# One loop body with staggered semaphore resets in place of 16 unrolled repeats, in a DMA-bound log-softmax gradient

One NeuronCore of a Trainium2 chip. The metric is the device time of one execution in microseconds, the median of several; times are compared within one chip.

## What is computed

```python
# y, dy: (8, 1024, 8192) float32
softmax_x = np.exp(y)
sum_dy = np.sum(dy, axis=-1, keepdims=True)
return dy - softmax_x * sum_dy
```

The 8192 rows are taken as 32 groups. In a group each of 128 partitions holds 2 neighbouring rows of 8192 elements, 64 KB, so one group of one tensor is a transfer of 8.39 MB. The kernel reads 537 MB and writes 268 MB.

## The kernel before

Two groups make a repeat, and there are 16 repeats, written out by a Python loop. Group g works in buffer x0, group g + 1 in x1. The y of the first lies in the upper part of one buffer y_t, the y of the second in its lower part, which overlaps the first. All transfers are issued by SyncE, in this order.

```python
def load_dy(g, x):
    nc.sync.dma_start(out=x[:], in_=dy_v[g])

def load_y(g, at, lo, hi):
    nc.sync.dma_start(out=y_t[:, at + lo : at + hi], in_=y_v[g][:, lo:hi])

# sums(x): VectorE sums row 0 of each partition, ScalarE row 1
# compute(...): in three pieces a row, ScalarE exp in y_t, VectorE x = y_t * s + x

for g in range(0, G, 2):
    load_dy(g, x_ts[0])                       # x0      64 KB a partition
    load_y(g, SHIFT, 0, W)                    # y       64 KB
    s_t = sums(x_ts[0])
    for r in range(R):
        compute(x_ts[0], s_t, SHIFT, r, PIECES_A)
    load_dy(g + 1, x_ts[1])                   # x1      64 KB
    s_t = sums(x_ts[1])
    for r in range(R):
        load_y(g + 1, 0, r * D, (r + 1) * D)  # first, second half of y, 32 KB each
        compute(x_ts[1], s_t, 0, r, PIECES_B)
    for j in range(2):
        nc.sync.dma_start(out=out_v[g + j], in_=x_ts[j][:])   # store of x0, store of x1
# ... cut: shapes, pools, launch
```

## Time and profile before

| | before |
|---|---|
| time | 1867.33 us (1866.91 to 1867.59, 4 runs) |
| bytes through the data queue | 805.31 MB, 432 GB/s over the span |
| busy share of VectorE, ScalarE | 46%, 37% |
| share of the 16 DMA engines' span that packets took | 99.8% |

Read it from the bottom row up: where the DMA engines have no idle time, the busy shares of the compute engines say nothing about the time, and the question for any change is whether it lets the DMA queue run dry. The lines are in the prediction.

Beside the views, the trace holds every DMA packet (start, duration, size). A row of 64 KB is one packet, and each of the 16 DMA engines carries 8 rows of a transfer. A packet does not name its engine: I follow an engine from the end of one packet to the start of the next, and a transfer's end on each engine is marked by a packet of 4 bytes. From these I work out, for each transfer, what the engines lost in it: the time from the end of the transfer before to its own end, mean over the engines, less what an undisturbed transfer takes (19.32 us with rows of 64 KB, 9.68 us with rows of 32 KB). This number, "lost in a transfer", is used throughout. In the kernel before it is 0.18 us for a whole repeat (repeats 1 to 14).

### The profile page before, as it was taken

The page shows a single profiled execution, that of the slowest core. Times are in us where ns is not written, and L with a number is a line of the kernel's source. Part 1 is how long each engine was busy: PE and PEld are TensorE (multiplying, and loading weights), DVE is VectorE, ACT ScalarE, POOL GpSimd, SP SyncE. Part 2 cuts the span into 40 slices and gives each one's busy share as a digit, 9 for nine tenths or more (in the row PEclk, how much of TensorE's full clock was granted, in tenths as well). Part 3 has the DMA queues.
Part 4 walks back from the last instruction along what each step waited for, and adds up shares of the span by engine and source line. Part 5 has one row for each costly group of instructions (what it writes and reads, how often), then busy time and mean ns, then how long its engine had stood idle before and what let it go on. Part 6 is the DMA issues. An engine that isn't in the chain of part 4 may idle for free.

```text
span 1866.1 us, 843 instructions
## 1 busy us (share of the span) xinstructions
DVE 857.9 (46%) x256; ACT 689.3 (37%) x257; POOL 0.2 (0%) x4
## 2 busy tenths in 40 slices
DVE  2907429074290742807328073280732806338163
ACT  2606326063260532605326053260523605235152
POOL 0000000000000000000000000000000000000000
DMA  9999999999999999999999999999999999999998
GB/s 427 427 427 427 431 444 429 427 434 443 427 434 438 425 435 442 428 429 431 440 431 430 438 427 436 437 440 427 430 438 435 428 437 428 438 435 434 434 428 386
DMA packets 16134, 805.36 MB, mean 432 GB/s; under 512 B 1792, under 2 KB 1792, under 8 KB 1792
## 3 DMA queue, kind: packets, MB, share of 16 engines
q1 hardware_dynamic: 16128, 805.31, 99.8%
q14 instruction: 6, 0.05, 0.0%
HBM read 536.87 MB, written 268.44 MB: 432 GB/s over the span
## 4 chain that ended last, share of the span: by engine, by line
DMA 65%; DVE 14%; another core or an unknown queue 10%; ACT 9%; issue 0%; DVEq 0%; ACTq 0%; SPq 0%
DMA x<-in_dy_dram 31%; DMA out_dram<-x 30%; DVE x L74 14%; ACT x L60 6%; ACT y_t L73 3%; DMA y_t<-in_y_dram 3%; DVEq L121 0%; ACTq L121 0%; SPq L52 0%; ACTq L73 0%; ACTq L60 0%
## 5 line engine op out<-in xcount | busy, mean ns | idle before, releaser
L74 DVE SCALAR_TENSOR_TENSOR x<-y_t,s_t,x 128x1024 f32<-128x1024 f32 (+2 forms) x192 | 579.4, 3059 | 257.5 <-ACT y_t L73 257.5
L57 DVE TENSOR_REDUCE s_t<-x 128x1 f32<-128x8192 f32 x32 | 277.8, 8682 | 721.9 <-DMA x<-in_dy_dram 721.9
L73 ACT ACTIVATE y_t<-y_t 128x1024 f32<-128x1024 f32 (+2 forms) x192 | 460.1, 2466 | 280.0 <-DMA y_t<-in_y_dram 280.0
L60 ACT ACTIVATE x<-x 128x8192 f32<-128x8192 f32 x32 | 225.0, 7030 | 863.2 <-DMA x<-in_dy_dram 863.2
L60 ACT ACTIVATION_READ_ACCUMULATOR x<-x 128x1 f32 x32 | 6.0, 187 | 0.0
L61 DVE TENSOR_SCALAR s_t<-second_t 128x1 f32<-128x1 f32 x32 | 4.6, 143 | 0.0
L60 ACT ACT_TABLE_LOAD x1 | 1.3, 1283 | 0.7 <-PEq L110 0.7
L110 POOL MEMSET const-uint8-127<- 128x1 uint8 x1 | 0.1, 102 | 0.0
L110 POOL MEMSET const-bfloat16-1.0<- 128x1 bf16 x1 | 0.1, 101 | 0.0
L110 POOL MEMSET const-float32-0.0<- 128x1 f32 x1 | 0.1, 98 | 0.2 <-issue 0.2
L110 POOL MEMSET const-float32-1.0<- 128x1 f32 x1 | 0.1, 98 | 0.0
## 6 DMA issues: line engine op xcount, KB each, us to landing
y_t<-in_y_dram SPq DMA_DIRECT2D x32, 4096.0 KB, 22.1
x<-in_dy_dram SPq DMA_DIRECT2D x32, 48.4
out_dram<-x SPq DMA_DIRECT2D x32, 32.6
y_t<-in_y_dram SPq DMA_DIRECT2D x16, 57.5
```

The lines of the kernel that those rows point to most:

```text
L57: nc.vector.tensor_reduce(out=s_t[:, 0:1], in_=x[:, :D], axis=mybir.AxisListType.X, op=ALU.add, negate=True)
L60: nc.scalar.activation(x[:, D:], x[:, D:], COPY, accum_out=second_t[:])
L61: nc.vector.tensor_scalar(out=s_t[:, 1:2], in0=second_t[:], scalar1=-1.0, scalar2=None, op0=ALU.mult)
L73: nc.scalar.activation(y_t[:, ys], y_t[:, ys], EXP)
L74: nc.vector.scalar_tensor_tensor(out=x[:, xs], in0=y_t[:, ys], scalar=s_t[:, r : r + 1], in1=x[:, xs], op0=ALU.mult, op1=ALU.add,)
L110: nc = _bacc.Bacc("TRN2", target_bir_lowering=False, num_devices=1)
```

## The change

The 16 repeats become one body, repeated by a branch on a register. Semaphores are reset stage by stage while the engines run: the body has four stages, and no engine enters a stage before all have reported the stage two back as done. The two `previous_stage_wait` lines make ScalarE and VectorE report one stage earlier than they otherwise would. The intent is a program of about a sixteenth of the length that runs as fast.

```diff
-    for g in range(0, G, 2):
+    with tc.For_i(0, G, 2, iteration_sync="staggered") as g:
         load_dy(g, x_ts[0])
         load_y(g, SHIFT, 0, W)
+        tc.stage_boundary()
+
+        for engine in (mybir.EngineType.Activation, mybir.EngineType.DVE):
+            tc.previous_stage_wait(engine)
         s_t = sums(x_ts[0])
         for r in range(R):
             compute(x_ts[0], s_t, SHIFT, r, PIECES_A)
         load_dy(g + 1, x_ts[1])
+        tc.stage_boundary()
+        for engine in (mybir.EngineType.Activation, mybir.EngineType.DVE):
+            tc.previous_stage_wait(engine)
         s_t = sums(x_ts[1])
         for r in range(R):
             load_y(g + 1, 0, r * D, (r + 1) * D)
             compute(x_ts[1], s_t, 0, r, PIECES_B)
+        tc.stage_boundary()
         for j in range(2):
             nc.sync.dma_start(out=out_v[g + j], in_=x_ts[j][:])
```

What the diff does not show, and the built program does: the store of x1 now waits for the semaphore that the store of x0 raises when it has landed.

## The prediction

> **What bounds the kernel now.** I read the page first (spans, slices, queues), then the DMA queue's own waits, then the timeline of one repeat, then the chain.
>
> ```profile
> span 1866.1 us, 843 instructions
> DVE 857.9 (46%) x256; ACT 689.3 (37%) x257; POOL 0.2 (0%) x4
> DMA  9999999999999999999999999999999999999998
> ...
> q1 hardware_dynamic: 16128, 805.31, 99.8%
> ```
>
> No engine is half busy, and the DMA row is 9 in all slices but the last; the one data queue's packets fill 99.8% of the 16 DMA engines' span. 805.31 MB in 1866 us is 432 GB/s. So the kernel is bound by the DMA engines, and only something that lets them go idle, or changes the bytes, can move the time. The bytes stay.
>
> One repeat (two groups) moves 6 x 8.39 MB: dy into x0, y, dy into x1, two half loads of y, store of x0, store of x1. All go through one queue, in the order of issue. In the trace's DMA packets a 64 KB row takes 2.418 us on its engine and the next starts at once (2.414 us from start to start), so an 8.39 MB transfer (8 rows per engine) takes 8 x 2.414 = 19.3 us. Six are 115.9 us; consecutive repeats in the trace end 116.06 to 116.9 us apart (the first later). The rest are small stalls that hit all engines at once.
>
> What matters is how early each transfer is queued before the one ahead of it runs out:
>
> ```profile
> 166.63 9.25 SPq L67 DMA_DIRECT2D y_t<-in_y_dram  x2
> ...
> 179.69 30.23 SPq L95 DMA_DIRECT2D out_dram<-x  x2
> ...
> 217.48 0.34 SPq L52 DMA_DIRECT2D x<-in_dy_dram  x1
> ...
> 236.90 0.33 SPq L52 DMA_DIRECT2D x<-in_dy_dram  x1
> ```
>
> This is the timeline of the second repeat, SyncE alone (start, duration, and two issues merged in a row). The store of x0 is issued at 179.69, the store of x1 ends its issue at 179.69 + 30.23 = 209.92. The next load of x0 starts at 217.48, released by the landing of the store of x0. So the store of x1 stood in the queue 7.6 us before its predecessor landed. It is the smallest reserve of the repeat. For the others: the first half of y is queued at 166.63 and the load ahead of it lands about 178.2 (11.6 us); the load of x0 is queued at 217.48 and the store ahead lands at 236.90 (19.4 us).
>
> ```profile
> SPq L67 <- DMA y_t<-in_y_dram: 615.0, 16, 39.7
> SPq L95 <- DVE x L74: 526.6, 32, 30.0
> SPq L52 <- DMA out_dram<-x: 386.4, 30, 18.5
> SPq L67 <- DVE x L74: 260.4, 32, 8.6
> ```
>
> These are the queue's own waits. **All 32 stores wait for VectorE**, none for a DMA: no store waits for another. The 30 waits on a store are loads into a buffer that is still being written out.
>
> The chain shows that these waits follow one another with no hole that the DMA engines feel:
>
> ```profile
> 62.52 38.28 DMA out_dram<-x
> 100.81 0.02 issue
> 100.82 38.71 DMA x<-in_dy_dram
> ```
>
> **What the Trainium skill says.**
> - "DMA: Bandwidth & Descriptors", Anatomy of one DMA: a DMA costs about 2.0 us fixed beside its bytes (fitted on GpSimd's path), mostly because the semaphore moves only when the last byte is confirmed; DMA engines don't wait on semaphores, the issuing sequencer does. The trace agrees in size: the first load is issued at 0.73 us and its last engine lands at 22.45, 21.72 us for 19.31 us of rows: 2.41 us fixed.
> - Same page, Latency and other measured facts: about 600 ns to the first byte from SyncE. The trace: the issue ends at 0.73 + 0.38 = 1.11, the first packets start at 1.74, 0.63 us later; the last of the 16 engines starts at 2.39.
> - "Advanced Engine Details and Errata", Control Flow Timing: a branch about 51 ns, compare-and-branch about 108 ns. The kernel before has no loop, so its trace can't show it.
> - "Runtime: NRT & Kernel Launch", Instruction fetch mechanics: a taken branch whose target isn't among the two resident blocks of 256 instructions stalls for a fetch. The loop body is some 20 to 40 instructions per engine, so I expect none after the first pass.
>
> **The change part by part.** The built program of the changed kernel holds the body once, with the same operations and shapes in the same order per engine and per queue. It adds:
>
> (a) *Loop control.* Per repeat and engine one add, one compare-and-branch, about ten semaphore instructions, an address instruction ahead of each of SyncE's DMAs. On SyncE the branch lies right after the store of x1 is issued, with a whole 19.3 us transfer running: free. On ScalarE and VectorE it lies between the end of one repeat's work (about 209 us in the timeline above) and 256 us, when x0 has landed: free. ScalarE's table load moves into the loop, 16 x 1.28 us (one in the page now, 1283 ns), in the same idle stretch: free. Before the first DMA there is one more barrier and a few semaphore sets: I put 1 us for it, once, a guess.
>
> (b) *Stage waits.* SyncE may not enter a stage until all engines have reported two stages back. Load of x1 after both stores have landed: the store of x1 it waited for anyway. Half loads of y after x0 and y have landed and after ScalarE and VectorE have reported stage 0, which the change makes them do at the head of stage 1; so the half loads still wait for VectorE's second piece. (If they reported only at the head of stage 2, the load would slip by some 13 us and eat its 11.6 us reserve. That is what this placement is for.) Stores after x1 has landed and both engines have finished x0: both were so before (178.2, and 179.7 for VectorE). So nothing here is on the path: 0 us.
>
> (c) *One new wait.* In the built program the store of x1 waits for the full count (16) of the semaphore that the store of x0, just ahead, raises. It didn't before. I read it as caution: with a register as group number the two destinations can't be told apart. So the store of x1 is issued only when the store of x0 has landed. At that moment nothing else is queued: the reserve goes from 7.6 us to below zero, and all 16 DMA engines run dry once per repeat.
>
> Cost of one dry spell, on the engine that ends last: last packet's end to its landing, 0.36 us (store of x0 in the first two repeats: 0.367 and 0.361); waking SyncE 0.02 us (an "issue" row above) and one more instruction between wait and issue, about 0.1; issue to the last engine's first packet, 2.39 - 0.73 = 1.66 us; filling the pipeline, 0.39 us (that engine's first row took 2.81 instead of 2.42). Sum 2.5 us if a store starts as the first load did. A store reads from SBUF and may fill faster, by up to the 0.39 us, and the first DMA of a program may be colder: 2.1 to 2.5. Against it, engines that drift apart (0.4 us apart in the first repeat, 1.1 us by the fourth) now wait for the slowest every repeat: 0.1 more. I take **2.4 us x 16 repeats = 38 us**. It is not hidden: VectorE is done 7.6 us earlier.
>
> Sum: 1867.5 + 38 + 1 = **1906 us**, 2.1% more.
>
> **The rivals.**
> - *Everything hidden.* If the new wait costs no more than a fraction of a microsecond (engines refilled quickly, say 0.6 us), 16 x 0.6 + 1 gives 1878 us. For it: 99.8% busy, and all stage waits have reserves. Against it: the queue can't be refilled before the landing, and the trace's only start from idle cost 2.4 us.
> - *A stage wait becomes the path.* If reports come later than I read them, the half loads of y slip to VectorE's end of x0: 1 to 2 us more per repeat, together 1920 to 1940 us. Against it: the order of decrement and wait in the built program.
> - *Branch fetches or slower address set-up* on SyncE, some us per repeat: they lie behind a 19.3 us transfer, so no change (1906), except set-up between landing and issue; 0.5 us there would give 1914.
> - *A gain:* a shorter program fetches fewer instructions, but the page's instruction queue has 0.05 MB in all, 0.0% of the time. Nothing to win.
>
> **Range and chances.** The sum hangs on one figure, 16 times the dry spell. 1.9 us gives 1899, 2.9 us gives 1915; with a little for the rest the range is 1896 to 1917. The 2% line is at 1867.5 x 1.02 = 1904.8, a dry spell of 2.27 us, just below my 2.4. So slower by over 2% has 0.58, within 2% 0.41, faster 0.01.
>
> **What would show it right or wrong.** Right: the queue's own waits show half of the stores' waits on a store rather than on VectorE, about 6 to 8 us each (from VectorE's end of x1 to the landing); the data queue's share falls from 99.8% to about 97.9%; in the packets all engines are idle together about 2 us between the two stores and nowhere else; repeats are about 118.5 us apart; busy times of VectorE and ScalarE unchanged but for 16 table loads. Wrong: a second idle stretch elsewhere in the repeat, above all ahead of the half loads of y (a stage wait); or no idle stretch between the stores (the wait isn't the bound); or the idle stretch is there but well under 2 us, and the kernel stays within 2%.

## The result

1919.18 us (1918.63 to 1919.38, 4 runs) against 1867.33: 2.8% slower. The ratio is 1.0277, 95% interval 1.026 to 1.0295. The predicted range ended at 1917.

The page of the changed kernel:

```profile
span 1917.4 us, 2048 instructions
DVE 859.4 (45%) x256; ACT 708.6 (37%) x272; POOL 0.2 (0%) x4
DMA  9999999999999999999999999999999999999999
...
q1 hardware_dynamic: 16128, 805.31, 98.5%
```

Same bytes, same work on VectorE; ScalarE has 16 table loads now (15 x 1.28 = 19.2 us more). The DMA row still shows 9 everywhere: a slice is 48 us wide, and a hole of 1.3 us in it can't be seen. The queue's share is the line that tells, and it fell only from 99.8% to 98.5%, while the time rose by 2.8%. So idle time is about half of the loss, and the other half hides in packets that took longer.

The queue's own waits (line of the waiting instruction, what ended the wait, us in total, times, longest):

```profile
SPq L83 <- DMA y_t<-in_y_dram: 608.3, 16, 39.3
SPq L103 <- DMA out_dram<-x: 598.0, 16, 37.7
SPq L83 <- DMA out_dram<-x: 284.9, 15, 19.1
SPq L67 <- DVE x L74: 250.8, 32, 8.4
SPq L83 <- DMA x<-in_dy_dram: 38.5, 16, 2.4
```

L103 is the stores. Before, all 32 of them waited for VectorE; now 16 wait 37 us each for a store. That wait runs from the issue of the store of x0 to its landing, so it swallows the one for VectorE. The L83 waits are the stage entries.

SyncE in the second repeat, and with it VectorE's last two pieces of x1 (timeline):

```profile
184.10 38.28 SPq L103 DMA_DIRECT2D out_dram<-x  x2
...
207.25 6.75 DVE L74 SCALAR_TENSOR_TENSOR x<-y_t,s_t,x 128x3072 f32<-128x3072 f32 x2 [0.30 <-ACT y_t L73]
...
223.14 0.35 SPq L52 DMA_DIRECT2D x<-in_dy_dram  x1
223.68 1.11 SPq L67 DMA_DIRECT2D y_t<-in_y_dram  x1
```

The pair of stores stretches from 184.10 to 222.38; before it ended 7.6 us ahead of the landing. VectorE is done with x1 at 214.0, 8 us before the store is issued. The chain through the same place (start, duration, what):

```profile
184.10 37.79 DMA out_dram<-x
221.89 0.02 issue
...
222.02 0.35 SPq L103
222.38 0.05 issue
...
222.90 0.03 SPq L129
...
223.14 40.02 DMA x<-in_dy_dram
```

It reads as a ledger of the dry spell, that is, the stretch in which the queue holds nothing and the engines idle. The store of x0 lands at 221.89, SyncE issues the store of x1 at 222.02, and between 222.38 and 223.14 lie the stage entry, the reset and the branches back to the head of the loop, 0.76 us in all, behind a transfer that is already queued. In the packets, the last engine ends the store of x0 at 221.54 and the first engine starts the store of x1 at 222.87: 1.33 us in which all 16 are idle. There is one such stretch in each of the 16 repeats (1.31 to 1.34 us), and nowhere else.

What was lost in each transfer, from the packets, ns, mean of repeats 1 to 14:

```
                 x0   y   x1  first half  second half  store x0  store x1   sum
before           12   5   26      23           99          8         2      175
changed         132  -2   -2      -1          885         -2      2579     3590
```

The difference is 3.4 us a repeat in these 14, and 51.9 us in the whole execution. 2.6 us is lost in the store of x1, as the dry spell would have it. But 0.8 us more is lost in the second half load of y, which is queued long before it starts and has no wait near it: the last two of its 8 rows on an engine take 1.50 and 1.80 us on average, where the others take 1.21. The prediction has nothing there.

The store of x1 itself is not made up as I thought either. Of its 2.58 us, 1.75 are the gap from one store's end to the next one's start on an engine (the 1.33 us, and the wait for the slowest engine), 0.1 lies in its first seven rows, and 0.72 in its **last** row. That row stalls where the engines turn from storing to loading, as the second half of y stalls where they turn from loading to storing. In the last repeat, where no load follows, the store of x1 lost 1.78 us instead.

### The profile page after: what moved, and what is told of

The parts are those of the page before. It is cut to its first block, busy times and chain, and to the rows that moved or that the text cites. A ratio compares the mean times of both kernels' runs of the same rounds, so it can differ in the third digit from the quotient of the medians.

```text
span 1917.4 us, 2048 instructions
## 1 busy us (share of the span) xinstructions
DVE 859.4 (45%) x256; ACT 708.6 (37%) x272; POOL 0.2 (0%) x4
## 3 DMA queue, kind: packets, MB, share of 16 engines
q1 hardware_dynamic: 16128, 805.31, 98.5%
## 4 chain that ended last, share of the span: by engine, by line
DMA 64%; another core or an unknown queue 11%; DVE 11%; ACT 8%; issue 3%; SPq 1%; ACTq 0%
DMA x<-in_dy_dram 31%; DMA out_dram<-x 30%; DVE x L74 11%; ACT x L60 6%; DMA y_t<-in_y_dram 3%; ACT y_t L73 3%; SPq L103 0%; SPq L67 0%; SPq L83 0%; SPq L52 0%; SPq L129 0%; ACTq L73 0%
```

## The experiments

Six questions, fifteen runs. All results were correct.

### Is the new wait the whole loss?

The loop without it. The two stores never touch the same rows, so the dependency may be declared away.

```diff
-        for j in range(2):
-            nc.sync.dma_start(out=out_v[g + j], in_=x_ts[j][:])
+        st = [nc.sync.dma_start(out=out_v[g + j], in_=x_ts[j][:]) for j in range(2)]
+        tc.declare_no_dep(st[1].ins, st[0].ins, reason="rows of group g + 1 are not rows of group g")
```

> The loop with one dependency declared away, so the store of x1 no longer waits for the landing of the store of x0; nothing else changes. Theory (the new wait is the whole loss): 1868 to 1870 us, that is the kernel before plus about 1.2 us for the later first issue (1.97 instead of 0.73 us); no stretch with all DMA engines idle; the stall at the end of the second half load of y shrinks over the first three repeats as it does before. Rival (the stage waits, semaphore resets or address instructions cost by themselves, the 0.9 us stall among them): 16 x 0.9 more, about 1883 us or above.

Measured 1867.87 us against 1867.34 for the kernel before on the same chip, ratio 1.0003 (0.9989 to 1.0016). Its page and the queue's waits:

```profile
span 1866.1 us, 2032 instructions
...
SPq L102 <- DVE x L74: 459.5, 16, 29.4
...
SPq L67 <- DVE x L74: 250.8, 32, 8.4
```

The stores wait for VectorE again, and all the rest of the loop (stage waits, resets, address instructions, branches, 16 table loads) costs nothing that these runs can show. The loss in the second half load is 0.54 us in repeat 0, 0.17 to 0.27 in repeats 1 to 7, and 0.03 from repeat 10 on. Its mean over repeats 1 to 14 is 0.13 us, against 0.10 in the kernel before and 0.89 in the changed one: it went with the wait.

The counter-test is the kernel before, unrolled, with that wait added and SyncE's order pinned (shortened; the loads are pinned too).

```diff
+        st = [tc.keep_in_program_order(nc.sync.dma_start(...)) for j in range(2)]
+        tc.add_manual_dep(st[1].ins, st[0].ins.name, <Sync>, reason=...)
```

> The unrolled kernel before, with SyncE's order pinned and one dependency added: the store of x1 waits for the landing of the store of x0. No loop. Theory (the wait is the whole loss, the stalls beside the idle stretch follow from it): 1917 to 1919 us, an idle stretch of 1.3 us per repeat, 2.5 us lost in the store of x1 and 0.9 us in the second half load of y in every repeat. Rival (only the 2.5 us come from the wait, the 0.9 us from the loop): 1905 to 1908 us.

Measured 1918.83 us, ratio 1.0274 (1.026 to 1.0288): the loop's time with no loop. Lost per repeat: 2.66 us in the store of x1, 0.88 us in the second half load. Its waits show the same pattern as the loop's:

```profile
SPq L97 <- DMA out_dram<-x: 607.1, 16, 39.1
SPq L52 <- DMA out_dram<-x: 300.0, 15, 20.2
```

**What follows.** The wait is necessary and enough for the whole loss, the part in the second half load included. The rival, that the loop's own instructions cause the 0.9 us, is out.

### Does the stall in the half load follow from the dry spell before it?

The same, with the wait in repeats 4, 8 and 12 alone (`if g in (8, 16, 24)` around the added dependency).

> As the last, but the wait stands in repeats 4, 8 and 12 alone (counted from 0). Theory (a dry queue puts the 16 DMA engines back in step, and in step they stall where they turn from loads to stores, until they have drifted apart): the second half load of y loses 0.8 to 1.0 us in repeats 5, 9 and 13, then less in the two after each; time 1867.3 + 3 x (2.5 + 1.3) = 1878 to 1880 us. Rival (the stall belongs to a dry spell of the same repeat or to the loop): no stall in repeats 5, 9, 13; 1875 us or less.

Measured 1878.67 us. Lost in the second half load of y and in the store of x1, ns, by repeat:

```
repeat         0   1   2   3     4    5   6   7     8     9  10  11    12   13   14   15
second half  780  56 206  93   208  972 195  24    43  1021  32  97    79  895  404  269
store x1      -2   7  -1  -2  2914   -2  43   4  2788    -2   4   1  4408   -2   -2   -2
```

Each dry spell is followed, a repeat later, by a stall of 0.9 to 1.0 us in the second half load, which is 0.03 to 0.40 us in the next. Repeat 0, which also starts from idle, has it too. So one dry spell costs itself and a stall some 97 us later; (1878.67 - 1867.34) / 3 is 3.8 us each.

### Does the wait cost anything where the queue is not empty?

The unrolled kernel with the wait, SyncE's order left to the scheduler, which puts the next repeat's whole load of y between the two stores.

> Unrolled, with the same wait of the store of x1 in every repeat, but the scheduler is left free and puts the next repeat's whole load of y ahead of that store, so 19.3 us of transfer stand in the queue while the store of x0 lands. Theory (the wait costs only because nothing is queued behind the store of x0): 1867 to 1870 us with one dry spell, at the end of the last repeat. Rival (a wait of a store on a store costs in itself, wherever it stands): 1900 us or more.

Measured 1884.03 us. SyncE in its third repeat (timeline):

```profile
305.74 0.34 SPq L94 DMA_DIRECT2D out_dram<-x  x1
332.32 0.33 SPq L67 DMA_DIRECT2D y_t<-in_y_dram  x1
337.64 0.34 SPq L94 DMA_DIRECT2D out_dram<-x  x1
```

The load of y is queued at 332.32, the store of x0 lands at 337.6 and releases the store of x1, and 19.3 us of y stand before it. The packets show a single all-idle stretch, at the end of the last repeat, so the wait as such is harmless; that half of the expectation held. But 17 us are lost all the same, so the other half, the time, failed. The packets place it: 1.06 us a repeat in the early load of y, at its turn into the store of x1, and 0.35 us more than before in the two half loads. The order now turns between loads and stores four times a repeat instead of twice. To tell order from wait, the same order without the wait (shortened: at the head of a repeat the load of y stays in the first repeat alone, and SyncE's order is pinned):

```diff
         for j in range(2):
+            if j and g + 2 < G:
+                load_y(g + 2, SHIFT, 0, W)
             nc.sync.dma_start(out=out_v[g + j], in_=x_ts[j][:])
```

> The order of flat_wait_y_first (next load of y ahead of the store of x1) without the wait. Theory: the 17 us that flat_wait_y_first lost come from its order, which turns between loads and stores four times a repeat instead of twice, and not from the wait: 1880 to 1886 us here too. Rival (the 17 us are the wait's): 1867 to 1870 us.

Measured 1882.53 us: so some 15 of the 17 us belong to the order. That turn lost 0.91 us on average, between 0.25 and 1.48 by repeat, in a queue that never ran dry. And with the early load in two halves:

> As flat_y_first, the early load of y in two halves of 32 KB rows. It asks whether the length of the rows ahead of the turn sets the stall (1.1 us before the store of x1 with 64 KB rows against 0.1 to 0.4 before the store of x0 with 32 KB rows, in flat_wait_y_first): if so, about 1870 to 1875 us; if not, the same as flat_y_first.

Measured 1871.01 us, and 0.07 us lost at that turn. Short rows ahead of this turn took the stall away, in this queue without dry spells.

### What does a dry spell cost by itself?

The store of x1 in two halves, the second waiting for the first.

> Unrolled, the store of x1 in two halves, the second waiting for the first as the first waits for the store of x0: two dry spells per repeat. The second adds idle time and restart alone, since the turn stalls are there already: 1.7 to 1.9 us each (1.3 all idle plus the engines' spread), so 1918.8 + 16 x 1.8 = 1947 us, 1943 to 1952. If a dry spell of a store after a store cost the whole 3.2 us that the loop lost, it would be 1970.

Measured 1945.69 us: (1945.69 - 1918.83) / 16 = 1.68 us for a second dry spell (another chip, whose kernel before took 1867.64 against 1867.34). That is the price of one wait for a landing with nothing queued behind, without the turns: the 1.3 us all idle and the engines' spread.

### What are the early reports worth?

The loop without the wait, and without the two `previous_stage_wait` pairs.

> The loop without the wait between the stores, and without the two early reports, so that ScalarE and VectorE report a stage done only two stages on. The half loads of y then wait for VectorE's end of x0 (about 179.7 in the timeline of before, 1.5 us after the load ahead has landed) and the store of x0 waits for VectorE's end of x1 (about 11 us after the second half load of y). I expect two dry spells per repeat, about 3 us and about 13 us, so 16 x 16 to 17 us more: 2120 to 2150 us. If the placement of the reports didn't matter it would stay at 1868 us.

Measured 2027.87 us, 8.6% slower. One of my two dry spells is there, and it is 9.1 us instead of 13; the other is not. The timeline of the second repeat:

```profile
169.64 14.32 ACT L73 ACTIVATE y_t<-y_t 128x1024 f32<-128x1024 f32 x6 [12.23 <-DMA y_t<-in_y_dram]
184.40 2.17 SPq L67 DMA_DIRECT2D y_t<-in_y_dram  x2
...
208.47 7.22 ACT L73 ACTIVATE y_t<-y_t 128x2048 f32<-128x2048 f32 x3 [2.55 <-DMA y_t<-in_y_dram]
...
216.12 4.08 SPq L98 DMA_DIRECT2D out_dram<-x  x2
```

The half loads are issued at 184.40, when **ScalarE** has ended x0 (183.96), not VectorE, and x1 lands only at about 189: a reserve of 4.6 us is left. The store of x0 is issued at 216.12, just after ScalarE has ended x1 (215.69). The engines ran out of work at 207.9 and restart at 217.0. So the reports' place matters, for the store more than for the half loads. In this run the second half load, after which the queue runs dry, lost 0.01 us: without a store right behind it there is no stall.

### Why do the engines stall at a turn?

My reading was that a dry queue puts the 16 DMA engines back in step, and that in step they get in one another's way where they all turn at once. In the kernel before they lie 0.4 us apart in repeat 0 and 3.7 us apart at the end, and the loss at the turn falls from 0.94 to 0.03 us meanwhile (not evenly: 0.37 in repeat 6). To set them apart at the start, one small load ahead of all, on 8 partitions and so on 8 engines:

```diff
+    nc.sync.dma_start(out=x_ts[1][0:8, 0:D], in_=dy_v[1][0:8, 0:D])
     for g in range(0, G, 2):
```

> The kernel before with one 8-partition half-row load at the start, so that 8 engines begin 1.2 us behind. Theory in step: the 0.9 us that the second half load of y loses in repeat 0, and the 0.4 us in repeat 1, fall to 0.2 us or less; time 1867 +- 1. Rival restart: they stay, time 1868.5.

Measured 1869.82 us, later by the load itself (x0 lands up to 3.6 us later). The second half load took 9.71 us in repeat 0, against 10.64 in the kernel before and 9.68 undisturbed: the stall is gone in this repeat. It isn't in all others: 0.19 us was lost in repeat 3 and 0.35 in repeat 8. Repeat 0 spoke for the reading. Then four attempts to do this after every dry spell, all on the unrolled kernel with the wait, each storing a few rows of x0 once more (the same bytes) ahead of the store of x1 (shortened):

```diff
         st = [ ...store of x0... ]
+        nc.sync.dma_start(out=out_v[g][0:8, 0:D], in_=x_ts[0][0:8, 0:D])   # or fewer columns, or other rows
         st.append( ...store of x1, with the wait... )
```

> Unrolled with the wait in every repeat, and after each dry spell SyncE stores 8 half rows of x0 once more (the same bytes), ahead of the store of x1: an 8-partition transfer should use 8 of the 16 DMA engines, so those run 1.2 us behind the other 8 through the following repeat. Theory in step (the stall at the turn from loads to stores, 0.9 us, and at the end of the store of x1, 0.7 us, come from all engines turning together): both shrink to 0.3 us or less while the idle stretch stays; the 1.2 us is paid once per repeat, so the time is 1910 to 1920 us. Rival restart (the stalls are what a restart from idle costs later, whatever the engines' distance): both stalls stay and 16 x 1.2 us is added, 1935 to 1940 us.

Measured 2001.66 us, a failed test. The rows took some 5.3 us each, not 1.2, and left two blocks of 8 engines some 4 us apart. The second half load lost 0.59 us, where flat_wait lost 0.88. At the turn to loads the last two rows of the store of x1 lost 0.39 us (0.73 in flat_wait), and the load of x0 behind them another 0.39 (0.12).

> As flat_wait_skew, but the extra stores take every fourth partition, so that the rows lie apart in SBUF, and are three: 8, 4 and 2 rows of 16 KB. The engines should then lie 0, 0.6, 1.2 and 1.8 us apart after each dry spell. In flat_wait_skew the 8 neighbouring rows took 5.3 us each instead of 1.2, so that run paid 16 x 5.2 us and left two blocks of 8 engines, each in step: no clean test. Theory in step: the stall at the turn to stores and the one at the end of the store of x1 both fall to 0.4 us or less; 1.8 us per repeat is paid and about 1.2 saved: 1923 to 1933 us. Rival restart: both stalls stay, 1918.8 + 29 = 1945 to 1950 us.

Measured 1957.24 us, a failed test again. The small stores were done before the store of x1 reached the engines, which therefore began it within 0.35 us of one another. The stalls were 0.7 us each, not far below flat_wait's 0.88 and 0.73. One thing this run shows beside its question: its 8 rows of 16 KB, every fourth partition, took 0.61 us each, while 8 neighbouring rows of 16 KB (flat_wait_lag16, below) took 2.3 to 3.0 us.

> As flat_wait_skew with rows of 8 KB instead of 32 KB. There the 8 neighbouring rows took 5.3 us, so here about 1.3 us, less the 0.5 us by which the store of x1 comes later: 8 engines lag the other 8 by about 0.8 us, as in skew_start. Theory in step: the stall at the turn to stores (0.9 us) and at the end of the store of x1 (0.7 us) fall to 0.4 us or less: 1904 to 1914 us. Rival restart: both stay, 1918.8 + 16 x 0.9 = 1930 to 1936 us.

Measured 1946.15 us. The lag was gone by the end of the store of x1 (all 16 engines within 0.55 us in the second repeat): no test.

> The same with rows of 16 KB: 8 engines lag by about 2.1 us. Theory in step: stalls fall to 0.4 us or less each, 1918.8 + 16 x (2.2 - 1.0) = 1938, 1930 to 1942 us. Rival restart: 1918.8 + 35 = 1951 to 1956 us.

Measured 1963.43 us, and here the engines did end the store of x1 in two blocks, at 244.8 to 245.0 and 246.1 to 246.5 us. The turn to stores lost 0.75 us. At the turn to loads the last two rows of the store of x1 lost 0.45 us and the load of x0 behind them 0.41, together what flat_wait lost there (0.73 and 0.12). So distance between two blocks doesn't remove the stalls; at most it moves a part of one. **The reading falls as I stated it.** The other suspect was the length of the rows ahead of the turn, after the run with half loads. With the dry spell kept, the second half load in two transfers of 16 KB rows, and the store of x1 in four:

> flat_wait with the second half load of y in two transfers of 16 KB rows (32 KB before). If the length of the rows ahead of the turn sets the stall, the 0.9 us falls to 0.45 or less: 1918.8 - 16 x 0.5 or more = 1903 to 1911 us, and the 0.7 us at the other turn stays. If row length doesn't matter: 1918 to 1920 us.

Measured 1919.62 us; the loss at the turn is 0.90 us, as with 32 KB.

> flat_wait with the store of x1 in four transfers of 16 KB rows (64 KB before), only the first of them with the wait. If row length sets the stall at the turn from stores to loads, the 0.7 us falls to 0.35 or less: 1907 to 1913 us, and the 0.9 us stays. If not: 1918 to 1920 us.

Measured 1924.63 us; the loss at that turn is 0.74 us, as with 64 KB. The time is longer than flat_wait's, so three more transfers are not free. So after a dry spell row length is not the cause either. That doesn't settle the turn of flat_y_first, where halving the rows did help.

**What is settled and what is open.** Shown: the stall lies at the turn between loads and stores when the other kind stands right behind; after a dry spell it is about 0.9 us into stores and 0.7 us into loads; it vanishes when no transfer of the other kind follows. In the order of the kernel before it is near nothing once the queue has run full for some ten repeats. That is not so in every order: flat_y_first never ran dry and lost 0.91 us a repeat at its added turn. Not shown: what in the state of the DMA engines, their queues or the memory decides it. After a dry spell neither the distance of the engines nor the row length alone does.

No version beat the kernel before. The loop without the wait equals it with a fraction of the program.

## Why the prediction was wrong

- *The bound* (the DMA engines, nothing else): right. The kernels' times follow the queue alone.
- *(a) Loop control is free:* right. The loop without the wait is within 0.2% of the kernel before. The first issue came 1.24 us later (1.97 against 0.73), for which I had put 1.
- *(b) Stage waits cost 0:* right for the kernel as it is. The aside on late reports was wrong in its detail: the half loads would slip by 7 us, not 13, and stay within their reserve; what late reports delay is the store of x0.
- *(c) The new wait, one dry spell a repeat:* the right cause, shown both ways, by its removal and by its addition.
- *The size of (c), "2.4 us x 16 repeats = 38 us":* **the step that failed.** The queue lost 3.4 us more per repeat than before (repeats 1 to 14), and 16 x 3.24 = 51.9 us in all. The missing term is the stall in the second half load of y, 0.8 us more than before, which the sum did not contain because it took the loss to lie only where the queue is empty. (The rest is small: 0.18 us in the store of x1 and 0.12 in the load of x0 behind it.) The trace of before had it in plain sight: 0.94 us in that transfer in repeat 0, the one repeat that started from an empty queue, and I set it aside as "small stalls".
- The 2.5 us I worked out for the store of x1 was measured as 2.58, but by two errors that cancel. I put 1.66 us from issue to the last engine's start and 0.39 for filling, taken from the first load of the program; the store started 0.85 to 1.0 us after its issue and filled in 0.06. In their place came 0.72 us at the turn to loads.
- *The rivals:* hidden (1878) and branch fetches were rightly set aside. The range, 1896 to 1917, varied the dry spell alone, and a term outside the list can't be covered by varying those on it. The rival of a stage wait (1920 to 1940) lies nearest to the measured 1919, but its mechanism is out: loop_nodep keeps all the stage waits and takes 1867.87.
- *The signs:* one idle stretch, between the stores and nowhere else, and the table loads were right, and so was the call of slower by over 2%, which had 0.58. The sizes were not: the engines idle 1.33 us together, not about 2; the queue's share is 98.5%, not 97.9; repeats are 119.5 us apart, not 118.5. Less idle time with more time lost is the mark of the stall, which shows as busy packets. "About 6 to 8 us each" for the stores' waits was wrong: the wait starts when the store of x0 is issued and shows as 37 us. Two small readings of the trace of before were off as well: by the fourth repeat the engines lay 1.3 us apart, not 1.1, and the repeats end 115.97 to 116.87 us apart, the longest not the first.

## What to carry to other kernels

When a loop replaces unrolled code, compare the waits of the built program transfer by transfer: a destination given by a register may be taken to overlap another, and a store may come to wait for a store. In a DMA-bound kernel, ask of each such wait what else stands in the queue when it is released; nothing meant here a dry spell of 1.7 us, and with the turns between loads and stores behind it, twice that. If the transfers are known to be disjoint, say so to the compiler; that alone brought the loop back from 1919 to 1868 us.

## What the Trainium skill lacked or had wrong

- "DMA: Bandwidth & Descriptors" gives the fixed cost of one DMA (about 2.0 us) and the rule to wait late; it doesn't say how much of that is lost when a queue of large transfers runs dry. Here: 1.2 to 1.4 us with all engines idle, 1.68 us per added dry spell (flat_wait_twice). It puts most of the fixed cost, measured on GpSimd's path, after the last byte; in the first load of the kernel before, issued by SyncE, 0.34 of the 2.41 us lay between the last packet's end and the landing.
- No page has a cost for turning between loads and stores in a full queue. Here, in the repeat after a dry spell, 0.9 us into stores and 0.7 us into loads; 0.03 us after ten repeats without one; 0.91 us on average at the turn of a load with 64 KB rows into a store, between two stores (flat_y_first), 0.07 us with 32 KB rows.
- "Advanced Engine Details and Errata", Control Flow Timing: the branches can't be told apart in these traces; a stage entry with its resets and the back edge together took 0.76 us on SyncE. "Runtime: NRT & Kernel Launch" on fetches after a taken branch: no stall appeared in a body this small.
- No page says that a store to a place given by a register may be made to wait for the store ahead of it. Here it cost 52 us of 1919.
